# A hybrid encoder block on one core: the wide and the narrow products of a weight chunk in two runs of eight, instead of in turn

## The chip, the cores and the metric

The kernel runs on one core of a Trainium2 chip. The metric is the device time of the whole program in microseconds (us), as the median of several runs; less is better. A trace of one profiled execution stands beside it.

## The reference

One layer of an encoder, for 256 tokens (`T`), 2048 channels (`D`) and float32 throughout. Every weight matrix is used once, for all 256 tokens.

```python
u   = rmsnorm(h)                                  # h is (256, 2048)
b_a, c_a, v_a, q, k, v, gl_a, gl_b = split(u @ w_in)          # 2048 -> 8704
y_a = (b_a * dwconv3(c_a * v_a)) @ w_out_a                    # 1024 -> 2048
y_b = windowed_attention(rope(q), rope(k), v, sink) @ w_o     # 1024 -> 2048, 16 heads, 4 kv heads
h   = h + (sigmoid(gl_a + b) * y_a + sigmoid(gl_b + b) * y_b) @ w_mix   # 2048 -> 2048
a, g = split(dwconv3(rmsnorm(h) @ w_up) + bias)               # 2048 -> 2 * 5632
h   = h + (silu(a) * g) @ w_down                              # 5632 -> 2048
return rmsnorm(h)
```

## The kernel before

**Tiles and splitting.** Channels lie on the 128 partitions and tokens along the free axis. A weight matrix is cut into blocks of 128 x 128. To keep float32's precision with TensorE's single-pass `fp32r` type, each operand is split into a high part and a remainder. An activation tile (`xs`, `ya_att`, `ms`, `hs`, `actA`, `actC`) holds both parts side by side, 256 columns high and 256 columns remainder, 512 in all. A weight block is split on the fly: ScalarE (ACT) casts the loaded `raw` to the high part `whi` (line 176), VectorE (DVE) subtracts it from `raw` to give the remainder `wlo` (line 187).

**The two products of a block.** TensorE (PE) multiplies each weight block twice into one PSUM bank `ps`. The *wide* product (line 215) takes `whi` against all 512 columns, high and remainder. The *narrow* product (line 216) takes `wlo` against the 256 high columns and adds to the first half of the bank. Each needs its own weights, so each is a weight load (LDWEIGHTS, shown as the engine PEld) and a matmul. Such a pair of products is the kernel's unit of work. A later step of ACT and DVE (`total`, `scaled` and the functions named `epi_...`) adds the two halves of the bank.

**Jobs and chunks.** A job is one output tile of 128 channels: `KT` = 16 pairs for a 2048-wide input, 8 for the two 1024-wide ones, 44 for `w_down`. `run` cuts the jobs into chunks of eight blocks of one job (`CH` = 8; the first jobs of the mix, up and down matrices are cut by four). A chunk's weights arrive in one DMA, are cast in one instruction and subtracted in one. `run` fetches six chunks ahead, casts three ahead and subtracts two ahead (`FETCH, HI, LO = 6, 3, 2`), with four `whi` and three `wlo` buffers. The first six jobs are different: they run together, block by block, six jobs to a chunk ("wide" groups in the code), so that work can begin when the first block has landed.

**Order of the work.** The schedule is written out by hand. Each engine executes its instructions in the order in which the Python code issues them. After every chunk `run_due` issues what is due then: the next step of every unfinished epilogue, and the attention, which `block` starts every five chunks or so (the scores `s` at lines 448 and 449, the transposes `ptp` at line 478, the products `av` with the values at line 491).

**Turned pairs.** Normally a pair is issued wide, then narrow. `turns` asks that, from the next 16-block job on, the pairs at certain distances (1, 5, 9 and 15; or 1 and 5, or 1 and 4 behind an attention block) are issued the other way round, narrow first. Around a turned pair the order is so wide, narrow, narrow, wide, wide, narrow. `turns` is called in the first group (chunk 4), behind each of the nine attention blocks from the second on, at chunk 78, and ten chunks after the second norm, which `r2` starts.

**The last job** has its own form: it takes only one half of the tokens in its "wide" product (from its second block on), and always issues the narrow product first. Behind it `finale` (line 695, tile `more`) runs 43 further products of 256 columns.

Of the kernel before, what the change touches and what calls it, by code (L numbers as in the profile page):

```python
# [16 lines left out]
T = 256  # L17
KT = D // P
# [33 lines left out]
def hybrid_block_kernel(ctx: ExitStack, tc: tile.TileContext, head, wide, xT, w_in, w_oa, w_o, w_mix, w_up, w_dn, vec, cst, out):  # L52
    nc = tc.nc
# [18 lines left out]
    def by_half(a):  # L72

        return a.rearrange("p (s h t) -> p h s t", s=2, h=2)
# [3 lines left out]
    def lazy(key, make):  # L78
        if key not in box:
            box[key] = make()  # L80
        return box[key]
# [3 lines left out]
    due, active = [], []  # L85
    now, count = [0], [0]

    def at(n, fn):
        due.append((n, count[0], fn))
        count[0] += 1  # L90

    def later(n, fn):
        at(now[0] + n, fn)

    def begin(fn, *args):
        g = fn(*args)
        if hasattr(g, "send") and next(g, 0) != 0:
            active.append(g)
# [6 lines left out]
    def finish():  # L105
        while active:
            step()

    def run_due():
        step()  # L110
        while True:
            ready = sorted(d for d in due if d[0] <= now[0])
            if not ready:
                return
            due.remove(ready[0])
            begin(ready[0][2])

    FETCH, HI, LO = 6, 3, 2

    TURNS, BEHIND = (1, 5, 9, 15), {"s": (1, 5), "ptp": (1, 5), "av": (1, 4)}
    pairs = [0]
    order = {"due": None, "turned": set()}

    def turns(which=TURNS):
        order["due"], order["turned"] = which, set()

    bank_tags = {}

    def run(groups):

        chunks = []
        for size, jobs, wide in groups:
            n = jobs[0][1]
            if wide:  # L140
                for k in range(n):
                    chunks.append((None, [(job, k) for job in jobs], wide))
                continue
            for k0 in range(0, n, size):
                k1 = min(n, k0 + size)
                for job in jobs:
                    chunks.append((job[0][:, k0:k1, :], [(job, k) for k in range(k0, k1)], None))
        raws, his, los, banks = {}, {}, {}, {}

        def pieces(c):  # L150

            n = len(chunks[c][1])
            return ((0, 2), (2, n)) if c < 3 else ((0, n),)

        def fetch(c):
            w, blocks, pre = chunks[c]
            if pre is not None:
                raws[c] = pre(0, c)
            else:
                raw = wpool.tile([P, CH, P], F32, tag="raw", name="raw", bufs=5)  # L160
                nc.sync.dma_start(raw[:, : len(blocks), :], w)
                raws[c] = lambda a, b, raw=raw: raw[:, a:b, :]


        def high(c):
            _, blocks, pre = chunks[c]
            if pre is not None:
                pre(1, c)
            (_, _, _, _, *halves), k0 = blocks[0]
            if halves:  # L170
                last = lazy("last", lambda: cpool.tile([P, FT, P], F32R, tag="B", name="last"))
                his[c] = last[:, k0 : k0 + len(blocks), :]
            else:
                his[c] = wpool.tile([P, CH, P], F32R, tag="whi", name="whi")
            for a, b in pieces(c):
                nc.scalar.copy(his[c][:, a:b, :], raws[c](a, b))  # L176
            if pre is not None:
                pre(2, c)

        def low(c):  # L180
            _, blocks, pre = chunks[c]
            if pre is not None:
                pre(3, c)
            los[c] = wpool.tile([P, CH, P], F32R, tag="wlo", name="wlo", bufs=3)
            raw = raws.pop(c)
            for a, b in pieces(c):
                nc.vector.tensor_tensor(los[c][:, a:b, :], raw(a, b), his[c][:, a:b, :], op=ALU.subtract)  # L187

        nxt = 0
        for c, (_, blocks, _) in enumerate(chunks):  # L190
            while nxt <= c + FETCH:
                for fn, i in ((fetch, nxt), (high, nxt - FETCH + HI), (low, nxt - FETCH + LO)):
                    if 0 <= i < len(chunks):
                        fn(i)
                nxt += 1
            hi, lo = his.pop(c), los.pop(c)
            ended = []
            for i, (job, k) in enumerate(blocks):
                _, n, rhs, epi, *halves = job
                if k == 0:  # L200
                    tag = bank_tags.get(id(job))
                    pool = aps if tag else lin
                    banks[id(job)] = pool.tile([P, 2 * T], F32, tag=tag or "ps", name="ps")
                ps = banks[id(job)]
                a, last, half = rhs(k), k == n - 1, bool(halves and k)
                if order["due"] and n == KT:
                    order["turned"] = {pairs[0] + d for d in order["due"]}
                    order["due"] = None
                turned = half or pairs[0] in order["turned"]
                assert half or not turned or k  # L210
                pairs[0] += 1
                both = by_half(ps)[:, 0] if half else ps
                moving = by_half(a)[:, 0] if half else a
                products = [
                    lambda: nc.tensor.matmul(both, hi[:, i, :], moving, start=k == 0, stop=last and turned),  # L215
                    lambda: nc.tensor.matmul(  # L216
                        ps[:, 0:T], lo[:, i, :], a[:, 0:T], start=False, stop=last and not turned
                    ),
                ]
                for product in reversed(products) if turned else products:  # L220
                    product()
                if last:
                    ended.append(job)
            now[0] += 1
            run_due()
            for job in ended:
                begin(job[3], banks.pop(id(job)))
        finish()
# [44 lines left out]
    def new_r(name):  # L273
        rr["r"] = cpool.tile([P, T], F32, tag="r", name=name)
        return rr["r"]
# [152 lines left out]
    def epi_v(i, ps):  # L428
        v = p1.tile([P, T], F32, tag="vraw", name="vraw", bufs=2)
        yield from scaled(ps, v)  # L430

        for _ in range(3 + 3 * i):
            yield 1
        tp = aps.tile([P, 2, T], F32, tag="tp", name="vtp")
        for b in range(2):
            nc.tensor.transpose(tp[:, b, 0:P], v[:, b * P : (b + 1) * P], ident)
        yield 1
        nc.scalar.copy(vtok[:, :, i * P : (i + 1) * P], tp[:, :, 0:P])
# [82 lines left out]
    def after(n, epi):  # L521


        def go(ps):
            for _ in range(n):
                yield 1
            yield from epi(ps)

        return go

    def qk(i):
        return lambda ps: epi_qk(i, ps)

    def cv(j, what):
        return lambda ps: epi_conv(j, what, ps)


    first = [
        (None, KT, xr, qk(0)),
        (None, KT, xr, qk(1)),  # L540
        (None, KT, xr, after(1, lambda ps: epi_v(0, ps))),
        (None, KT, xr, after(1, lambda ps: epi_v(1, ps))),
        (None, KT, xr, after(2, cv(0, "c"))),
        (None, KT, xr, after(3, cv(0, "v"))),
    ]
    assert len(first) == WIDE
    for job, tag in zip(first[2:], ("tp2", "s0", "s1", "av")):
        bank_tags[id(job)] = tag
    at(4, turns)
    at(14, r1)  # L550
    groups = [(None, first, pre_x)]

# [12 lines left out]
    for t in range(10):  # L565

        def block(t=t):
            if t > 1:
                begin(att_out, t - 2)
            for e in range(2):  # L570
                if 0 < t < 9:
                    begin(att_turn, t - 1, e)
            for e in range(2):
                if t < 8:
                    begin(att_scores, t, e)
            if t:
                turns(BEHIND["s" if t < 8 else "ptp" if t < 9 else "av"])

        at(29 + 21 * t // 4, block)
    at(78, turns)  # L580

    def start_gates():
        p0.close()
# [64 lines left out]
    half = {}  # L648

    def r2():  # L650
        nc.scalar.preload_act_table_set("natural_log_exp_and_others")
        yield from inv_rms([acc2], new_r("r2"))
        later(10, turns)

    def epi_up(i, which, ps):
        c = i + which * FT
# [115 lines left out]
    jobs = [(w_dn[m], FT, act, lambda ps, m=m: epi_dn(m, ps)) for m in range(KT - 1)]  # L772
    outer_first(jobs + [(w_dn[KT - 1], FT, act, finale, True)], 2)
    run(groups)
    assert not due, due

# [96 lines left out]
```

## Time and profile before

| | us |
|---|---|
| median of 3 runs (lowest, highest) | 1331.14 (1331.09, 1331.62) |
| the profiled execution | 1332.0 |
| its span, first to last instruction | 1330.2 |
| PE busy, of the span | 1320.0 (99%) |
| DVE busy | 955.7 (72%) |
| ACT busy | 723.1 (54%) |
| POOL busy | 70.1 (5%) |

The 1.8 us between the profiled execution and its span lie ahead of the first and behind the last instruction. The granted TensorE clock is 0.998 of full speed on average. The ends of matmuls are modelled in the profile and overlap the next matmul, so a matmul's own duration says little here: what a product costs is read from one start to the next start. The data moved is 255.54 MB, 192 GB/s on average.

### The profile page before, as it was taken

Reading aid. Unit: us, or ns where it says so; the run is one execution under the profiler, and the core shown is the slowest. Engines: PE = TensorE matmul, PEld = TensorE weight load, DVE = VectorE, ACT = ScalarE, POOL = GpSimd, SP = SyncE. Lnnn points to the kernel's source line nnn. Section 1 sums busy time; section 2 is a strip of 40 time slices with the busy share of each in tenths; the row PEclk is TensorE's granted clock in tenths of the full one; section 3 lists DMA queues with packets and bytes.
Section 4 is the critical chain, followed back from the end, with each engine's and each line's share of the span. In section 5 each row is a group of like instructions: output and inputs, shape, how many; then the busy total and the mean of one; then the engine's idle time right before and its main releaser. Section 6 shows DMA issues by size and latency. Waiting matters only on the chain.

```text
span 1330.2 us, 20480 instructions
## 1 busy us (share of the span) xinstructions
PE 1320.0 (99%) x7686; PEld 1161.4 (87%) x7686; DVE 955.7 (72%) x1508; ACT 723.1 (54%) x1151; POOL 70.1 (5%) x66
## 2 busy tenths in 40 slices
PE   9999999999999999999999999999999999999997
PEld 8888888888888888888888888888888888888886
DVE  7888777555557887668888888888888865445444
ACT  7667665555555545446555555555555545444442
POOL 0000000000000002430000000000000001111211
PEclk9999999999999999999999999999999999999999
DMA  8786545555555547547555555555555557666663
GB/s 309 234 243 200 199 158 175 182 191 190 191 189 190 190 143 236 188 141 235 190 190 190 191 190 190 190 191 190 191 190 190 174 153 236 194 186 183 197 191 104
DMA packets 76676, 255.54 MB, mean 192 GB/s; under 512 B 8864, under 2 KB 9248, under 8 KB 76576
## 3 DMA queue, kind: packets, MB, share of 16 engines
q1 hardware_dynamic: 76144, 253.44, 59.1%
q8 instruction: 60, 0.98, 0.3%
q10 hardware_dynamic: 432, 0.79, 0.2%
q14 instruction: 40, 0.33, 0.1%
HBM read 248.16 MB, written 2.10 MB: 188 GB/s over the span
## 4 chain that ended last, share of the span: by engine, by line
PE 99%; DVE 0%; ACT 0%; POOLq 0%; issue 0%; DVEq 0%; ACTq 0%
PE ps L215 63%; PE ps L216 33%; PE av L491 1%; PE ptp L478 1%; PE warm L311 0%; PE s L448 0%; PE s L449 0%; PE more L695 0%; POOLq L868 0%; DVE y L737 0%; DVE r L729 0%; DVE x L702 0%; PE nps L259 0%; ACT ln L719 0%; PE nps L717 0%
## 5 line engine op out<-in xcount | busy, mean ns | idle before, releaser
L187 DVE TENSOR_TENSOR wlo<-raw,whi 128x1024 fp32r<-128x1024 f32 (+3 forms) x493 | 568.0, 1154 | 314.4 <-PE ps L216 222.2
L176 ACT CAST whi<-raw 128x1024 fp32r<-128x1024 f32 (+3 forms) x493 | 488.2, 992 | 326.4 <-PE ps L215 187.7
L215 PE MATMUL ps<-hs,whi 128*128 128x512 f32 x1408 | 488.2, 391 | 0.0
L216 PE MATMUL ps<-hs,wlo 128*128 128x256 f32 x1408 | 393.6, 280 | 0.0
L215 PE MATMUL ps<-xs,whi 128*128 128x512 f32 x1088 | 377.4, 392 | 0.0
L215 PEld LDWEIGHTS ps<-hs,whi 128*128 128x128 f32 x1408 | 263.0, 187 | 57.4
L216 PE MATMUL ps<-xs,wlo 128*128 128x256 f32 x1088 | 300.6, 280 | 0.0
L216 PEld LDWEIGHTS ps<-hs,wlo 128*128 128x128 f32 x1408 | 266.1, 189 | 0.4
L215 PEld LDWEIGHTS ps<-xs,whi 128*128 128x128 f32 x1088 | 202.2, 188 | 42.9 <-issue 0.4
L216 PEld LDWEIGHTS ps<-xs,wlo 128*128 128x128 f32 x1088 | 205.8, 189 | 2.4
L245 ACT COPY evb<-ps 128x256 f32<-128x256 f32 x188 | 70.0, 373 | 197.9 <-PE ps L216 194.2
L215 PE MATMUL ps<-actC,whi 128*128 128x512 f32 x420 | 146.2, 391 | 0.0
L216 PE MATMUL ps<-actC,wlo 128*128 128x256 f32 x448 | 124.4, 280 | 0.0
L215 PEld LDWEIGHTS ps<-actC,whi 128*128 128x128 f32 x420 | 78.5, 187 | 17.2
L215 PE MATMUL ps<-ya_att,whi 128*128 128x512 f32 x256 | 88.8, 391 | 0.0
L215 PE MATMUL ps<-ms,whi 128*128 128x512 f32 x256 | 88.8, 391 | 0.0
L216 PEld LDWEIGHTS ps<-actC,wlo 128*128 128x128 f32 x448 | 84.8, 189 | 0.0
L215 PE MATMUL ps<-actA,whi 128*128 128x512 f32 x240 | 83.8, 391 | 0.0
L249 DVE TENSOR_TENSOR evt<-ps,evb 128x256 f32<-128x256 f32 x178 | 74.4, 418 | 0.7 <-ACT evb L245 0.7
L216 PE MATMUL ps<-ya_att,wlo 128*128 128x256 f32 x256 | 71.7, 280 | 0.0
L216 PE MATMUL ps<-ms,wlo 128*128 128x256 f32 x256 | 71.7, 280 | 0.0
L216 PE MATMUL ps<-actA,wlo 128*128 128x256 f32 x256 | 70.9, 280 | 0.0
(144 smaller groups left out, 1050.3 us busy)
## 6 DMA issues: line engine op xcount, KB each, us to landing
raw<-in_w_up_dram SPq DMA_DIRECT2D x170, 512.0 KB, 4.1
raw<-in_w_in_dram SPq DMA_DIRECT2D x124, 512.0 KB, 3.6
raw<-in_w_dn_dram SPq DMA_DIRECT2D x70, 512.0 KB, 4.4
raw<-in_w_mix_dram SPq DMA_DIRECT2D x26, 512.0 KB, 4.3
raw<-in_w_dn_dram SPq DMA_DIRECT2D x36, 256.0 KB, 2.7
raw<-in_w_oa_dram SPq DMA_DIRECT2D x16, 512.0 KB, 3.2
raw<-in_w_o_dram SPq DMA_DIRECT2D x16, 512.0 KB, 3.2
raw<-in_wide_dram SPq DMA_DIRECT2D x14, 512.0 KB, 5.2
```

Source lines behind the costliest of these rows:

```text
L176: nc.scalar.copy(his[c][:, a:b, :], raws[c](a, b))
L187: nc.vector.tensor_tensor(los[c][:, a:b, :], raw(a, b), his[c][:, a:b, :], op=ALU.subtract)
L215: lambda: nc.tensor.matmul(both, hi[:, i, :], moving, start=k == 0, stop=last and turned),
L216: lambda: nc.tensor.matmul(ps[:, 0:T], lo[:, i, :], a[:, 0:T], start=False, stop=last and not turned),
L245: nc.scalar.copy(b, ps[:, T : 2 * T])
L249: nc.vector.tensor_tensor(dst, ps[:, 0:T], b, op=ALU.add)
L478: nc.tensor.transpose(tp[:, b, n * P : (n + 1) * P], p[:, n, b * P : (b + 1) * P], ident)
L491: nc.tensor.matmul(o[64 * e : 64 * e + 64, 0:T], vtok[:, b, v0 : v0 + HD], pT[e][:, b, :], start=b == 0, stop=b == 1)
```

## The change

Within a chunk of one job, the wide products of all its blocks are issued first, and then the narrow products of all of them: eight wide, eight narrow (four and four where a chunk has four blocks). The chunks of the first six jobs, which hold blocks of different jobs, and the last job keep their pairs in turn. `turns`, its tables and its four calls are taken out, so no pair is turned any more outside the last job. The bank's accumulation ends with the last narrow product, as before.

```diff
-    TURNS, BEHIND = (1, 5, 9, 15), {"s": (1, 5), "ptp": (1, 5), "av": (1, 4)}
-    pairs = [0]
-    order = {"due": None, "turned": set()}
-    def turns(which=TURNS):
-        order["due"], order["turned"] = which, set()
...
+            apart = blocks[0][0] is not blocks[-1][0] or len(blocks[0][0]) > 4
+            narrow = []
             for i, (job, k) in enumerate(blocks):
...
-                if order["due"] and n == KT:
-                    order["turned"] = {pairs[0] + d for d in order["due"]}
-                    order["due"] = None
-                turned = half or pairs[0] in order["turned"]
-                assert half or not turned or k
-                pairs[0] += 1
...
-                products = [
-                    lambda: nc.tensor.matmul(both, hi[:, i, :], moving, start=k == 0, stop=last and turned),
-                    lambda: nc.tensor.matmul(
-                        ps[:, 0:T], lo[:, i, :], a[:, 0:T], start=False, stop=last and not turned
-                    ),
-                ]
-                for product in reversed(products) if turned else products:
-                    product()
+                def wide(i=i, both=both, moving=moving, first=k == 0, last=last and half):
+                    nc.tensor.matmul(both, hi[:, i, :], moving, start=first, stop=last)
+
+                def part(i=i, ps=ps, a=a, last=last and not half):
+                    nc.tensor.matmul(ps[:, 0:T], lo[:, i, :], a[:, 0:T], start=False, stop=last)
+
+                if half:
+                    part(), wide()
+                elif apart:
+                    wide(), part()
+                else:
+                    wide()
+                    narrow.append(part)
                 if last:
                     ended.append(job)
+            for part in narrow:
+                part()
             now[0] += 1
...
-    at(4, turns)
...
-            if t:
-                turns(BEHIND["s" if t < 8 else "ptp" if t < 9 else "av"])
...
-    at(78, turns)
...
-        later(10, turns)
```

The order of PE's instructions at two places shows it. The first is behind the second attention block: the last score products of that block (`s_...` are the score banks, `kh` and `kl` the two parts of the keys) and the first pairs of the job that follows. Before:

```order
L448 MATMUL s_1109<-kh,qs 128x256
L449 MATMUL s_1109<-kl,qs 128x256
L215 MATMUL ps<-xs,whi 128x512
L216 MATMUL ps<-xs,wlo 128x256 x2
L215 MATMUL ps<-xs,whi 128x512 x2
L216 MATMUL ps<-xs,wlo 128x256
L215 MATMUL ps<-xs,whi 128x512
```

The same place after the change, where line 202 issues the wide and line 205 the narrow products:

```order
L442 MATMUL s_1109<-kh,qs 128x256
L443 MATMUL s_1109<-kl,qs 128x256
L202 MATMUL ps<-xs,whi 128x512 x8
L205 MATMUL ps<-xs,wlo 128x256 x8
L202 MATMUL ps<-xs,whi 128x512 x8
```

The turned pair (two narrow, then two wide in a row) is gone, and the job's sixteen pairs are four runs of eight.

The second place is on PE too, in the first jobs of the up matrix, where chunks have four blocks and the second norm's sum (`nps`) stands between two of them. The waits that an instruction carries stand in brackets: on ACT for `whi`, on DVE for `wlo`. Before:

```order
L259 MATMUL nps<-acc_105,ones 128x256 [waits Pool_49]
L215 MATMUL ps<-hs,whi 128x512 [waits Activation_49]
L216 MATMUL ps<-hs,wlo 128x256 [waits DVE_49]
L215 MATMUL ps<-hs,whi 128x512
L216 MATMUL ps<-hs,wlo 128x256
```

After:

```order
L253 MATMUL nps<-acc_105,ones 128x256 [waits Pool_49]
L202 MATMUL ps<-hs,whi 128x512 [waits Activation_49]
L202 MATMUL ps<-hs,whi 128x512 x3
L205 MATMUL ps<-hs,wlo 128x256 [waits DVE_49]
L205 MATMUL ps<-hs,wlo 128x256 x3
L202 MATMUL ps<-hs,whi 128x512 [waits Activation_49]
```

The wait for `wlo` now stands behind all wide products of the chunk, instead of behind the first. In all of PE's order after the change there are 417 runs of eight wide and as many of eight narrow, and 59 of four each. The instructions of ACT, DVE, POOL and SP, their order and the engines they wait for are the same as before.

## The prediction

> **What bounds the kernel now.** I read the page first: how busy each engine is, the granted clock, and the chain of work that ended last.
>
> ```profile
> span 1330.2 us, 20480 instructions
> PE 1320.0 (99%) x7686; PEld 1161.4 (87%) x7686; DVE 955.7 (72%) x1508; ACT 723.1 (54%) x1151; POOL 70.1 (5%) x66
> PEclk9999999999999999999999999999999999999999
> PE 99%; DVE 0%; ACT 0%; POOLq 0%; issue 0%; DVEq 0%; ACTq 0%
> ```
>
> PE is busy without a break, at the full granted clock, and the chain that sets the end runs through PE alone. Whether PE waits for anybody is told by its list of waits, which has two rows:
>
> ```profile
> PE warm L311 <- DVE wm L304: 1.5, 1, 1.5
> PE nps L717 <- ACT sq L716: 1.0, 1, 1.0
> ```
>
> One is at the start and one in the tail; no pair of products waits. So the time is the number of pairs times what a pair takes. The number comes from the page's groups of narrow products (line 216, one per pair):
>
> ```profile
> L216 PE MATMUL ps<-hs,wlo 128*128 128x256 f32 x1408 | 393.6, 280 | 0.0
> L216 PE MATMUL ps<-xs,wlo 128*128 128x256 f32 x1088 | 300.6, 280 | 0.0
> L216 PE MATMUL ps<-actC,wlo 128*128 128x256 f32 x448 | 124.4, 280 | 0.0
> L216 PE MATMUL ps<-ya_att,wlo 128*128 128x256 f32 x256 | 71.7, 280 | 0.0
> L216 PE MATMUL ps<-ms,wlo 128*128 128x256 f32 x256 | 71.7, 280 | 0.0
> L216 PE MATMUL ps<-actA,wlo 128*128 128x256 f32 x256 | 70.9, 280 | 0.0
> ```
>
> They add up to 3712 pairs. The time of one I read from the windows, over the long undisturbed stretch of the up and down matrices, and from a piece of the timeline (start, duration, engine), PE's rows and then PEld's:
>
> ```profile
> 640.00:1300.00 660.00, 660.00 (x3809) 581.95 (x3808) 472.83 (x726) 348.86 (x512) 31.88 (x27) 1.00 0.61 190
> ```
>
> ```profile
> 300.10 0.28 PE L216 MATMUL ps<-xs,wlo 128*128 128x256 f32 x1
> 300.22 0.39 PE L215 MATMUL ps<-xs,whi 128*128 128x512 f32 x1
> 300.45 0.28 PE L216 MATMUL ps<-xs,wlo 128*128 128x256 f32 x1
> ...
> 300.10 0.19 PEld L215 LDWEIGHTS ps<-xs,whi 128*128 128x128 f32 x1
> 300.22 0.19 PEld L216 LDWEIGHTS ps<-xs,wlo 128*128 128x128 f32 x1
> ```
>
> 3809 matmuls in 660.00 us are 1904 pairs with one at the edge: 346.6 ns each. From wide to narrow it is 0.23, from narrow to wide 0.12. The load of the next weights starts together with the matmul that runs, so each product, wide or narrow, has exactly one weight load beside it. That stays so in either order.
>
> **The change, part by part.** *What moves.* No product, load, DMA, cast or subtraction is added or removed. 96 pairs of the first group (6 jobs of 16) and 44 of the last job keep their order; 3712 - 96 - 44 = 3572 pairs are regrouped, in 417 chunks of eight and 59 of four (417 x 8 + 59 x 4 = 3572). With PE as the only bound, the question is what a wide product costs behind a wide one and a narrow one behind a narrow one, against 346.6 for the two in turn.
>
> *Narrow behind narrow.* The last job and the products behind it are already such a run: all have 256 columns.
>
> ```profile
> 1310.09 0.28 PE L215 MATMUL ps<-actC,last 128*128 128x256 f32 x1
> 1310.21 0.28 PE L216 MATMUL ps<-actC,wlo 128*128 128x256 f32 x1
> ...
> 1315.01 1.96 PE L695 MATMUL more<-actA,last 128*128 128x256 f32 x15
> ```
>
> 15 of them take 1.96 with the last one's 0.28, so (1.96 - 0.28) / 14 = 0.120 each, and the rows of the last job are 0.12 apart as well. A narrow product in a run costs 120 ns.
>
> *Wide behind wide.* No run of wide products at this clock stands in the trace, only two in a row, at the turned pairs. The chain in order of time lists 30 such pieces, 28 with 0.47 for the two and two with 0.46; the first, the last one of the first group, and the last:
>
> ```profile
> 15.78 0.47 PE ps L215 x2
> ...
> 20.69 0.47 PE ps L215 x2
> ...
> 623.42 0.47 PE ps L215 x2
> ```
>
> That is 235 ns for one. A turned place in the timeline:
>
> ```profile
> 15.38 0.40 PE L216 MATMUL ps<-xs,wlo 128*128 128x256 f32 x2
> 15.61 0.63 PE L215 MATMUL ps<-xs,whi 128*128 128x512 f32 x2
> 16.08 0.28 PE L216 MATMUL ps<-xs,wlo 128*128 128x256 f32 x1
> 16.20 0.39 PE L215 MATMUL ps<-xs,whi 128*128 128x512 f32 x1
> 16.42 0.28 PE L216 MATMUL ps<-xs,wlo 128*128 128x256 f32 x1
> ```
>
> 15.61 to 16.08 is again 0.47 for two. But these places are short, and the products around them are not at their steady pace, so I look for what a steady pace can be. The trace has a second one, in the first 24 pairs, which are strictly in turn:
>
> ```profile
> 8.79 0.40 PE L215 MATMUL ps<-xs,whi 128*128 128x512 f32 x1
> 9.02 0.28 PE L216 MATMUL ps<-xs,wlo 128*128 128x256 f32 x1
> 9.13 0.40 PE L215 MATMUL ps<-xs,whi 128*128 128x512 f32 x1
> 9.37 0.28 PE L216 MATMUL ps<-xs,wlo 128*128 128x256 f32 x1
> 9.48 0.40 PE L215 MATMUL ps<-xs,whi 128*128 128x512 f32 x1
> 9.72 0.28 PE L216 MATMUL ps<-xs,wlo 128*128 128x256 f32 x1
> 9.85 0.40 PE L215 MATMUL ps<-xs,whi 128*128 128x512 f32 x1
> ```
>
> Three pairs take 9.85 - 8.79 = 1.06, or 353.3 ns each; behind the turned pairs it is 346.6. So the same order has two paces, and an even step fits all three steady figures: 346.7, 1060 and 120 ns are 52, 159 and 18 steps of 6.67 ns. My reading, which no row proves, is that a run settles to whole steps. A run of one kind of product repeats product by product, so each must then take whole steps: the narrow one 18 (120 ns, as measured, though 0.117 is what is left of 346.6 behind a wide one's 0.23), the wide one 34 (226.7), 35 (233.3) or 36 (240). The rows are nearest to 35: alone between narrow ones a wide product takes 0.23, behind a wide one 0.235. So I take 233.3 + 120 = 353.3 ns per regrouped pair, 6.7 more than now.
>
> *The sum.* 3572 x 6.7 ns = +23.9 us. Each chunk has one step from wide to narrow and one from narrow to wide, which now cost 0.23 and 0.117; if these stay, a chunk gets up to 6.7 ns back, 476 x 6.7 ns = 3.2 us; I take half, -1.6. In the first group the turned pairs go; the slow pace of 353.3 then lasts on from the last turn there, at 20.69 us, to the sum of the first norm:
>
> ```profile
> 40.19 0.59 PE L259 MATMUL nps<-sq,ones 128*128 128x256 f32 x2
> ```
>
> Those are some 55 pairs x 6.7 ns = +0.4. The turned pairs behind attention go with the regrouping and have no term of their own. Together +22.7 us. Against the profiled execution (1332.0 us, span 1330.2) this is 1354.7; the median of the runs is 0.9 lower, so 1353.8.
>
> *Bounds.* The low end for a wide product in a run is its 0.230 between narrow ones: 350.0 per pair, 3.4 x 3572 = +12 us, with the smaller terms +11: 1342. The high end is 0.235, as behind a wide one: 355 per pair, 8.4 x 3572 = +30 us, with the first group's 0.4: 1362. No pause by another engine is in it, for these reasons:
>
> ```profile
> DVE wlo L187 <- PE ps L216: 226.0, 210, 2.1
> ACT whi L176 <- PE ps L215: 187.7, 156, 2.2
> ```
>
> The casts and subtractions wait for PE to free a buffer, not the other way round. `whi` is now freed after eight wide products, 8 x 0.12 = 0.96 us before the chunk's end; `wlo` is needed later and freed at the same end. I cost both at nothing, since what hides them is PE's own work, and a slower PE gives them more room. DMA follows them and is at 0.61 of its time in that window. The attention's instructions keep their places between chunks.
>
> *A rule of the skill.* The row gives 0.23 and 0.12 in turn. The Trainium skill, "TensorE: Matmul & The Clock Gate", section "Back-to-back issue gap", has columns / 2.4 plus 2.5 ns for an isolated matmul at the full clock, 216 ns for 512 columns and 109 for 256, whatever the order. An estimate by it is 325 ns for a pair in any order, and no change; the trace disagrees with the level by 22 ns, so I take no term from it.
>
> **Rivals.** *No change.* Each product pays the same for its weight load whatever stands beside it. Then a wide one costs 346.6 - 120 = 226.6 in a run (34 steps), and the sum is nil: 1331. For it: the load beside every product, and that 226.7 and 120 are whole steps and fill the fast pair exactly. Against it: all 30 pieces of two wide ones are at 0.46 or 0.47, where it asks for 0.453.
>
> *Faster.* A wide product takes 0.22, as at 16.20 to 16.42, once its neighbours no longer disturb it, by its own stream alone. With 0.120 for the narrow one the pair is 0.340: -6.6 x 3572 = -24 us, 1307. The mechanism is the longer time of a wide product that hides its successor's load, now in runs; the place is the seven wide-to-wide steps of each chunk, and it decides once such a step is under 226 ns. For it speaks that row alone. Against it: one such step per turned place, while the next and the one before are over 0.23. By the skill's rule above, the wide step would be 216 and, with the row's 120 for the narrow one, the time an estimated 39 us less.
>
> *PE waits.* If the narrow products found `wlo` late, or the next chunk's `whi` came late, PE would show waits; 0.1 us per chunk would be 476 x 0.1 = +48 us. The two rows above speak against it, and neither buffer is needed earlier than now by more than the first chunk's pace. It is hardly likely.
>
> **How the numbers follow.** The forecast, slower by the pace of wide runs (1342 to 1362): 0.62. Between it and no change (1334 to 1342): 0.05. No change: 0.13. Faster: 0.17. Slower still, waits among it: 0.03. The range 1330 to 1362 takes in the first three, 0.80. Within 0.2% (2.7 us, about what a measurement of this kernel can tell from no change) is the no-change case. So: slower 0.70, same 0.13, faster 0.17. The likeliest case is 1353.8.
>
> **What would show it.** In the timeline after, seven wide products in a run should stand 0.23 to 0.235 apart and seven narrow ones 0.12; a chunk of eight should take 2.82 us instead of 2.77; the window from 640 to 1300 us should hold about 3737 matmuls, not 3809. PE should still be at 99%, with no wait on `whi` or `wlo`; the casts should start earlier in a chunk. The first group should stay at 1.06 for three pairs up to 40 us. I am wrong if the wide steps are at 0.227 or less, or if chunks begin with a pause.

## The result and the profile after

The changed kernel takes 1340.66 us in the median (1340.49 to 1341.31), before 1331.38 in the same comparison: ratio 1.007, 95% interval 1.0058 to 1.0082. It is slower by 9.3 us. I had forecast slower, by 22.7 us.

The page of the changed kernel:

```profile
span 1338.7 us, 20480 instructions
...
PE 1328.5 (99%) x7686; PEld 1167.1 (87%) x7686; DVE 961.6 (72%) x1508; ACT 734.5 (55%) x1151; POOL 59.1 (4%) x66
...
PE 99%; DVE 0%; ACT 0%; POOLq 0%; issue 0%; DVEq 0%; ACTq 0%
```

It is the same work, and PE holds 99% of the chain as before. PE's list of waits has the same two rows as before (lines are shifted by the edit). Below them stands the row of the casts from the list of all engines: they wait less for PE, 152.0 us in all instead of 187.7.

```profile
PE warm L305 <- DVE wm L298: 1.5, 1, 1.5
PE nps L706 <- ACT sq L705: 1.0, 1, 1.0
```

```profile
ACT whi L166 <- PE ps L202: 152.0, 147, 2.2
```

So the 9.3 us lie in the steps from one product to the next. The window over the up and down matrices:

```profile
640.00:1300.00 660.00, 660.00 (x3782) 580.39 (x3782) 477.87 (x726) 356.80 (x508) 18.95 (x26) 1.00 0.59 188
```

3782 products instead of 3809 are 349.0 ns per pair instead of 346.6: 2.4 ns more, and 2.4 x 3572 = 8.6 us of the 9.3. The timeline of some chunks in the gates shows it by product (line 202 wide, line 205 narrow; a merged row has the start of its first product and the duration from there to the end of its last):

```profile
299.40 2.00 PE L202 MATMUL ps<-xs,whi 128*128 128x512 f32 x8
301.24 1.12 PE L205 MATMUL ps<-xs,wlo 128*128 128x256 f32 x8
302.19 2.00 PE L202 MATMUL ps<-xs,whi 128*128 128x512 f32 x8
304.04 1.11 PE L205 MATMUL ps<-xs,wlo 128*128 128x256 f32 x8
304.99 2.00 PE L202 MATMUL ps<-xs,whi 128*128 128x512 f32 x8
```

Two chunks take 304.99 - 299.40 = 5.59, or 2.795 each, where eight pairs in turn take 2.773. Eight wide products take 1.84 to 1.85, 230 to 231 ns each; eight narrow ones 0.95, 119 each. The chain in order of time gives a finer figure for the down matrix. It lists one run per job of 44 pairs, and of the twelve rows from the first to the last I show both ends:

```profile
1128.53 1.86 PE ps L202 x8
...
1297.63 1.86 PE ps L202 x8
```

Eleven jobs take 1297.63 - 1128.53 = 169.10, or 15.373 each. In turn it would be 44 x 346.6 = 15.250. The job has six runs of wide products (five of eight, one of four), so a run costs 0.123 / 6 = 20 ns on average, three of the prediction's steps of 6.67 ns.

### The profile page after: what moved, and what is told of

Same layout as the page of the kernel before. It is cut to its first block, busy times and chain, and to the rows that moved or that the text cites. A ratio compares the mean times of both kernels' runs of the same rounds, so it can differ in the third digit from the quotient of the medians.

```text
span 1338.7 us, 20480 instructions
## 1 busy us (share of the span) xinstructions
PE 1328.5 (99%) x7686; PEld 1167.1 (87%) x7686; DVE 961.6 (72%) x1508; ACT 734.5 (55%) x1151; POOL 59.1 (4%) x66
## 4 chain that ended last, share of the span: by engine, by line
PE 99%; DVE 0%; ACT 0%; POOLq 0%; issue 0%; DVEq 0%; ACTq 0%
PE ps L202 63%; PE ps L205 33%; PE av L485 1%; PE ptp L472 1%; PE warm L305 0%; PE s L442 0%; PE s L443 0%; PE more L684 0%; POOLq L857 0%; DVE y L726 0%; DVE r L718 0%; DVE x L691 0%; PE nps L253 0%; ACT ln L708 0%; PE nps L706 0%
## 5 line engine op out<-in xcount | busy, mean ns | idle before, releaser
L166 ACT CAST whi<-raw 128x1024 fp32r<-128x1024 f32 (+3 forms) x493 | 487.0, 990 | 218.8 <-PE ps L202 152.0
L202 PE MATMUL ps<-hs,whi 128*128 128x512 f32 x1408 | 353.8, 392 | 0.0
L202 PE MATMUL ps<-xs,whi 128*128 128x512 f32 x1088 | 282.6, 393 | 0.0
L205 PEld LDWEIGHTS ps<-hs,wlo 128*128 128x128 f32 x1408 | 192.9, 190 | 14.3
L205 PE MATMUL ps<-hs,wlo 128*128 128x256 f32 x1408 | 197.3, 282 | 0.0
L205 PE MATMUL ps<-xs,wlo 128*128 128x256 f32 x1088 | 165.2, 282 | 0.0
L205 PEld LDWEIGHTS ps<-xs,wlo 128*128 128x128 f32 x1088 | 153.6, 190 | 9.8
L205 PE MATMUL ps<-actC,wlo 128*128 128x256 f32 x448 | 67.4, 282 | 0.0
L275 ACT ACTIVATE up<-evs,vt 128x256 f32<-128x256 f32 x88 | 53.0, 602 | 21.5 <-DVE evs L365 17.0
L365 DVE TENSOR_TENSOR evs<-evt,r 128x256 f32<-128x256 f32 x120 | 51.0, 425 | 4.1
L202 PEld LDWEIGHTS ps<-ya_att,whi 128*128 128x128 f32 x256 | 46.0, 189 | 8.2
```

What stands on the lines that cost most here:

```text
L202: nc.tensor.matmul(both, hi[:, i, :], moving, start=first, stop=last)
L205: nc.tensor.matmul(ps[:, 0:T], lo[:, i, :], a[:, 0:T], start=False, stop=last)
L275: nc.scalar.activation(dst, src, AF.Identity, bias=bias, scale=w1)
L365: nc.vector.tensor_tensor(dst, t, rr["r"], op=ALU.mult)
```

## The experiments

Six kernels, all written from the changed one. (The diffs shown for runs of four and of two are against the kernel in turn, and the remarks behind `#` are mine.) Three theories were on record. A: the steady pace in runs (the time per product once it no longer changes) is the same as in turn, and what costs is each *return* from narrow to wide products, a few whole steps, gone after a few wide products. B: each product of a run costs a little more, however long the run. C: the waits for `whi` and `wlo`, once per chunk, are what costs.

**Only the second half of the change: in turn, without turned pairs.**

```diff
-                    wide()
-                    narrow.append(part)
+                    ops.append((wide, part))
...
-            for part in narrow:
-                part()
+            seq = []
+            for g in range(0, len(ops), RUN):          # RUN = 1: wide, narrow, wide, narrow, ...
+                seq += [w for w, _ in ops[g : g + RUN]] + [p for _, p in ops[g : g + RUN]]
...
```

> Only the second half of the change: all pairs in turn, no turned pairs, no runs. Theory A (a sequence of products settles to one of several paces in steps of 6.67 ns, and the turned pairs were there to get it out of the slow one): from the first attention block at about 75 us to the second norm at about 583 us the pairs keep the slow pace, 353.3 ns instead of 346.7, some 1440 pairs x 6.7 ns = +9.6 us against before, that is about 1341, as slow as the changed kernel. Rival (the pace has nothing to do with turned pairs): within 1 us of before, 1331.

Measured: 1340.64 in the median (five of six executions from 1339.98 to 1340.80, one at 1352.27) against 1331.55, +9.1. The ratio of the means, 1.0081 (1.0057 to 1.0106), has the one at 1352.27 in it; the medians give 1.0068. Windows of this kernel, and below them of before, in the middle of the slow stretch and behind it:

```profile
260.00:560.00 300.00, 300.00 (x1701) 260.51 (x1700) 200.68 (x291) 149.45 (x226) 17.38 (x17) 1.00 0.56 187
620.00:1300.00 680.00, 680.00 (x3925) 600.19 (x3925) 494.40 (x764) 360.63 (x533) 29.45 (x25) 1.00 0.60 190
```

```profile
260.00:560.00 300.00, 300.00 (x1733) 264.54 (x1732) 204.53 (x296) 152.21 (x229) 20.89 (x19) 1.00 0.57 190
620.00:1300.00 680.00, 680.00 (x3924) 599.54 (x3923) 489.39 (x752) 360.04 (x530) 31.88 (x27) 1.00 0.61 190
```

From 260 to 560 us 1701 products stand where before has 1733: 352.7 ns per pair, the slow pace. From 620 us on there is no difference. Between the two lies the sum of the second norm, and the timeline of this kernel shows the change of pace there, 1.06 for three pairs ahead of it and 1.04 behind:

```profile
598.15 0.40 PE L203 MATMUL ps<-hs,whi 128*128 128x512 f32 x1
...
599.21 0.40 PE L203 MATMUL ps<-hs,whi 128*128 128x512 f32 x1
...
602.75 0.59 PE L256 MATMUL nps<-acc,ones 128*128 128x256 f32 x2
...
617.05 0.39 PE L203 MATMUL ps<-hs,whi 128*128 128x512 f32 x1
...
618.09 0.39 PE L203 MATMUL ps<-hs,whi 128*128 128x512 f32 x1
```

So the turned pairs of before do work: they bring PE to the fast pace behind the attention, and without them it keeps the slow one until the second norm's sum. The changed kernel is as slow as this one for another reason. It loses in both stretches (1720 products from 260 to 560 us instead of 1733, 3782 from 640 to 1300 instead of 3809), this one only ahead of the norm; that the sums agree is chance.

**Runs of four.**

```diff
-    RUN = 1
+    RUN = 4                                            # W4 N4 W4 N4 in a chunk of eight
```

> As the changed kernel, but each chunk of eight goes four wide, four narrow, four wide, four narrow. Theory A (the steady pace in runs is the same as in turn, and each return from narrow to wide products costs whole steps: 20 ns where runs have eight, about 14 where they have four, as in the chunks of four of the changed kernel): 893 returns x 13.5 ns = +12 us against before, about 1343.5, 1402 ns for four pairs, with the second group of a chunk like the first. Rival B (each product in a run costs more, 2.5 ns per pair, whatever the run's length): +9, as the changed kernel, 1340.7. Rival C (the price is that of the waits for whi and wlo, once per chunk): 20 ns per chunk of eight, the second four wide products without a price, 1340.7.

Measured: 1345.08, ratio 1.0101 (1.0088 to 1.0114), +13.5. A and its size hold; B and C, which asked for the changed kernel's time, fall. Half of these groups begin inside a chunk, where no wait for `whi` or `wlo` stands, and they are no shorter (each line 203 row to the next):

```profile
699.99 1.09 PE L203 MATMUL ps<-hs,whi 128*128 128x512 f32 x4
...
701.40 1.09 PE L203 MATMUL ps<-hs,whi 128*128 128x512 f32 x4
...
702.80 1.09 PE L203 MATMUL ps<-hs,whi 128*128 128x512 f32 x4
...
704.21 1.09 PE L203 MATMUL ps<-hs,whi 128*128 128x512 f32 x4
```

Four pairs take 1.40 to 1.41, against 1.386 in turn. By the time of the whole, 13.5 us / 893 = 15 ns per return, and there are nearly twice as many returns as in the changed kernel.

**Runs of two.**

```diff
-    RUN = 1
+    RUN = 2                                            # W2 N2, four times in a chunk of eight
```

> As the changed kernel, but two wide, two narrow, and so on. Theory A (whole steps of 6.67 ns per return, priced by the excess of the first two wide products of a run, 6.6 and 9 ns over 226.7, less 7 ns at the first narrow): one step, 6.7 ns, per two pairs: 1786 x 6.7 = +12 us, about 1343.5 (two steps would be +24, 1355). Rivals B and C: +9, 1340.7.

Measured: 1336.94, ratio 1.004 (1.0027 to 1.0053), +5.4. All three expectations missed, A's by half. Timeline, wide rows:

```profile
699.90 0.62 PE L203 MATMUL ps<-hs,whi 128*128 128x512 f32 x2
...
700.59 0.63 PE L203 MATMUL ps<-hs,whi 128*128 128x512 f32 x2
...
701.29 0.63 PE L203 MATMUL ps<-hs,whi 128*128 128x512 f32 x2
...
706.17 0.63 PE L203 MATMUL ps<-hs,whi 128*128 128x512 f32 x2
```

From 699.90 to 706.17 are nine groups of two pairs, 0.6967 each, 3.4 ns over in turn. That is half a step. It fits whole steps only over two groups (1393.3 ns are 209 steps); A had taken one whole step for each group. So the price of a return is not the same for every length of run, and it cannot be added up from the first products of longer runs, as I had done.

**Runs of sixteen.** A chunk that follows narrow products of its own job begins with its narrow products.

```diff
+            seq = [[w for w, _ in ops], [p for _, p in ops]]
+            if ops:
+                if ended_narrow[0] and blocks[0][1]:   # not a job's first chunk
+                    seq.reverse()                      # W8 N8 | N8 W8 | W8 N8 | ...
+                    ended_narrow[0] = False
+                else:
+                    ended_narrow[0] = True
+            seq = seq[0] + seq[1]
...
```

> As the changed kernel, but a chunk that follows a narrow run within the same job begins with its narrow products: eight wide, sixteen narrow, sixteen wide, and so on. 292 wide runs instead of 476. Theory A (20 ns per return, paid off within the first five wide products): 271 x 20 + 21 x 14 = +5.7 us against before, about 1337. Rival B (2.5 ns per pair): +9, 1340.7. Rival C (per wait of a chunk): +9, 1340.7.

Measured: 1336.54, ratio 1.0037 (1.0025 to 1.0049), +5.0. A's 5.7 is near, B and C, at 9, fall. The timeline shows a whole run of each kind and the start of the next; the second row is the answer for a stretch that begins inside the wide run, and so has the start of its fifth product:

```profile
703.69 3.82 PE L203 MATMUL ps<-hs,whi 128*128 128x512 f32 x16
...
704.62 2.89 PE L203 MATMUL ps<-hs,whi 128*128 128x512 f32 x12
...
707.34 2.08 PE L206 MATMUL ps<-hs,wlo 128*128 128x256 f32 x16
709.26 0.63 PE L203 MATMUL ps<-hs,whi 128*128 128x512 f32 x2
```

The first four wide products take 704.62 - 703.69 = 0.93, 232.5 each; the other twelve 707.34 - 704.62 = 2.72, 226.7 each. So the steady pace of a wide run is 226.7 ns, 34 steps, and the loss sits at its beginning. The sixteen narrow ones take 709.26 - 707.34 = 1.92, 120 each; 226.7 + 120 is the 346.7 of a pair in turn.

**Fewer columns.** Two runs to see whether steps are real: all wide products of the regrouped chunks but a job's first take 508 or 504 columns instead of 512, so the last columns are left out of the sum.

```diff
...
+                    if first or half or apart:
+                        nc.tensor.matmul(both, hi[:, i, :], moving, start=first, stop=stop)
+                    else:                              # 504 in the second kernel
+                        nc.tensor.matmul(both[:, 0:508], hi[:, i, :], moving[:, 0:508], start=False, stop=stop)
...
```

> The changed kernel, but the wide products of the regrouped chunks, save the first of each job, take 508 columns instead of 512 (3359 products; four columns of the second half of the bank are left out of the sum). A column costs (226.7 - 120) / 256 = 0.417 ns. If a run of products settles to whole steps of 6.67 ns (my reading in the prediction): a wide product at its steady pace keeps 226.7 ns, and the time stays within 1.5 us of the changed kernel's 1340.7. If there are no steps: 225.0 ns, 3359 x 1.67 = -5.6 us, about 1335.

> As the run with 508 columns, but with 504 (eight columns left out). No steps: 223.3 ns for a wide product at its steady pace, -11 us, about 1329.5. Whole steps per single product: 226.7 (no change, 1340.7) or 220.0 (-22 us, 1318). Steps over a repeat of several products: 223.3 as a mean of different rows, which this run cannot tell from no steps by its time, only by its rows.

Measured: 1333.17 with 508 (ratio to before 1.0013, 1.0004 to 1.0023) and 1334.05 with 504 (1.0019, 1.0009 to 1.0029). By their times they decide nothing: against the changed kernel 7.5 and 6.6 us are gained, which is none of the values that I had set, and eight columns less gain no more than four. The rows of the kernel with 504 say why. Here is a chunk that has cut products only, and (second row, from a stretch that begins inside) its last five products:

```profile
702.10 1.98 PE L206 MATMUL ps<-hs,whi 128*128 128x504 f32 x8
...
702.78 1.29 PE L206 MATMUL ps<-hs,whi 128*128 128x504 f32 x5
...
703.91 1.12 PE L209 MATMUL ps<-hs,wlo 128*128 128x256 f32 x8
...
704.87 0.40 PE L204 MATMUL ps<-hs,whi 128*128 128x512 f32 x1
```

The last five take 703.91 - 702.78 = 1.13, 226 ns each: no less than with 512 columns, where 223.3 would follow from the columns. That speaks for steps. The whole chunk takes 704.87 - 702.10 = 2.77, as if in turn: with this width the second chunk of a job pays almost nothing for its return. So the gain is in the returns, not in the pace. The kernel with 508 does not bear out steps product by product:

```profile
702.90 1.99 PE L206 MATMUL ps<-hs,whi 128*128 128x508 f32 x8
704.72 1.11 PE L209 MATMUL ps<-hs,wlo 128*128 128x256 f32 x8
705.67 0.40 PE L204 MATMUL ps<-hs,whi 128*128 128x512 f32 x1
```

This chunk too takes 2.77, as if in turn, but its eight wide products take 704.72 - 702.90 = 1.82, 228 each on average. By the start times in the trace, in ns, the chunks of this form between 640 and 680 us go 232, 226, 223, 225, 230, 232, 233, 224: in runs of eight they reach no steady pace. Whole steps hold for the settled runs seen here, not for every product.

## Why the prediction was right or wrong

**The bound, right.** PE holds 99% of the chain, with no new wait and nothing on other engines: the added time lies between one PE product and the next.

**Narrow behind narrow, right.** I forecast 120 ns. It is 119 over a run of eight, because the first one is shorter; this is the run at 304.04 us, whole and from a stretch that begins inside it:

```profile
304.04 1.11 PE L205 MATMUL ps<-xs,wlo 128*128 128x256 f32 x8
...
304.15 1.00 PE L205 MATMUL ps<-xs,wlo 128*128 128x256 f32 x7
```

From the first to the second it is 0.11, and the other seven take 304.99 - 304.15 = 0.84, 120 each.

**Wide behind wide, wrong: this is the step that failed.** I took 233.3 ns, 35 steps, as the steady pace. It is 226.7, 34 steps, the value that the rival of no change had. Whole steps fit the settled runs, though why is not shown; the choice between 34 and 35 was made by the 30 pairs of wide products at turned places, which I had said myself are not at their steady pace. They show the beginning of a run (232 ns over the first four), not its pace. This term was +23.9; at the steady pace it is nil. My own sign of being wrong, wide steps at 0.227 or less, is what the long run shows.

**The corners, wrong in sign and size.** I gave each chunk back up to 6.7 ns for its two changes of kind, -1.6 in all. The whole loss is at the changes and in the few products behind them: 20 ns per run of eight, 417 x 20 ns = 8.3 us, and with the 59 runs of four at an assumed price between 13 and 20 ns, 9.1 to 9.5, around the measured 9.3. That slower came true is luck: the term that was to make it so is nil, and the loss comes from a term that I had with the other sign. No rival had a price per return; the pace of wide runs and the returns together would have given the time.

**The first group, wrong.** I had the slow pace last up to 40 us; in the profiled execution of the changed kernel it was not there.

```profile
8.30 0.39 PE L202 MATMUL ps<-xs,whi 128*128 128x512 f32 x1
...
9.34 0.39 PE L202 MATMUL ps<-xs,whi 128*128 128x512 f32 x1
```

Three pairs take 1.04 from the start on. In the kernel before, three pairs at this place took 1.06, though PE's products are the same up to there; what decides it is open. The term was 0.4.

**The rivals.** Faster: the steady wide step is 226.7, and not the 220 that this rival asked for. No steady run came down to the 216 ns that the Trainium skill ("TensorE: Matmul & The Clock Gate", section "Back-to-back issue gap") gives for an isolated matmul of 512 columns. (The estimate that I made with it comes to 346.6 - 336 = 10.6 ns per pair, 38 us, not 39.) Waits: none. No change: right on the pace and wrong on the sum. The range held the time only because it reached down to this rival: 1340.66 lies between 1334 and 1342, the stretch to which I had given 0.05.

**What stays open.** Why products settle to steps of 6.67 ns, and what makes a return cost 20 ns, some 15, 3.4 or almost nothing, was not tried; the runs show that it depends on the run's length and on the width of the products. The steps themselves rest on the settled runs here, and the 508 columns do not fit them product by product.

## What to carry to other kernels

Where PE is the bound and each product has its own weight load, do not count on a gain from putting equal products side by side: here the steady paces added up to the same (226.7 + 120 against 346.7 in turn), and each change from one kind to the other could cost time (20 ns per run of eight). Measure the pace of an order in a run that is long enough to settle (a dozen products or more was enough here), and price its beginning separately; the pairs of wide products at the turned places showed the beginning. And a piece of code that seems to do nothing, such as a few pairs in reverse, may hold PE in its fast pace, as it did here, at 9.1 us: look at the step from start to start before taking it out.

## What was not expected of the hardware

PE has more than one steady pace for the same instructions: 346.6 or 353 ns per pair in turn, kept for hundreds of us (the in-turn kernel, slow from 260 us at the latest up to the second norm's sum at 603 us, fast behind it). A wide product of 504 columns takes as long in a settled run as one of 512, 226 to 227 ns. And the time is not ordered by the length of runs: +5.4 us for two, +13.5 for four, +9.3 for eight, +5.0 for sixteen, against in turn with turned pairs.
